# The b projection of a gated convolution as seven-product pairs, in one chain of nine pairs with c and h

## The chip, the cores and the metric

The kernel runs on one core of one Trainium2 chip. The metric is the device time of one execution in microseconds, the median of several runs. One execution was also taken by the hardware profiler; all rows of the profile come from that one.

## The reference, cut to what matters

One decoder layer. 576 tokens (512 new positions of one prompt, and 8 sequences of 8 sample positions) of width 1024 are normalised and go through one wide projection `w_in`, whose 6144 columns are six parts of 1024. The change touches the first three, b, c and h:

```python
xn = rms_norm(h, g_mix[i])
z = xn @ w_in[i]
b, c, hc = z[..., :o1], z[..., o1:o2], z[..., o2:o3]
...
u = c * h
ext = jnp.concatenate([buf, u], axis=1)
y = sum(ext[:, k:k + T] * w_conv[k] for k in range(CONV_W))
return b * y, ext[:, -(CONV_W - 1):]
```

The product b * y is then projected by `w_out_conv`, gated, added to a pooled branch and projected again; an MLP of width 4096, a gated per-layer embedding and a last normalisation follow. Everything is float32.

## The kernel before, in words

**Layout.** Channels lie on the 128 partitions, tokens along the free dimension, in two halves of 288 (256 prompt and 32 sample tokens). There are NJ = 8 tiles of 128 channels, so a projection of 1024 columns is 8 output tiles, each summing over 8 input tiles. `xg` is the input times the gain; the per-token factor of the normalisation, `r1` (and `r1s`, its square, where c and h meet), is multiplied in after the matmuls.

**Precision.** A float32 operand is split into a high part, rounded to the matmul's type, and the remainder (`split`, lines 87 to 99): ScalarE makes `hi` (L93), VectorE `lo` (L94). A product is then three matmuls, hi x hi, hi x lo and lo x hi. Weights are loaded by SP into `raw` buffers (8 of them, `raw_tile`, L126 to L129), split into 7 pairs of weight buffers (`wsp`, NF = 7), and used in the order of one long list, `order`; `Stream` (L190) loads six items ahead of the splits, and splits as far ahead as the seven buffers allow.

**Plain product.** `product` (L118) makes one output tile from two list items (`unit`, each 128x512 of weights): 8 input tiles x 3 matmuls x 2 halves = 48 matmuls of 128x288, into two of six PSUM banks.

**Seven-product pair.** `Pair` (L155) takes two output tiles q and q + 4 with the two halves of the input channels and the two halves of the tokens as a 2 x 2 by 2 x 2 block product, done with seven quarter products in place of eight (the Strassen-Winograd form). The weight side needs seven matrices, the `forms` a, b, d, s0, s1, s2 and s3. Of these s1 and s0 are sums made by a DMA that adds into a loaded buffer: SP loads `c`, and POOL issues a second DMA that accumulates (`summed`, L162 to L165). s2 and s3 are made by VectorE from buffers that are already there (L184, L186), and all seven are split. The token side (`xo`, an `Operand`) is prepared once. `quarter` (L382) is one quarter product, 4 x 3 = 12 matmuls. `pairs_of` (L436 to L499) runs a chain of n pairs: per pair the products t2, t3, t1, then b21 (whose corner result is ready first and goes to `corner`), then the first product of the next pair (`begin`) or a `filler`, then t4 and b22, after which `finish` gets the other three results. VectorE joins the products out of PSUM in five additions (L461, L463, L465, L492, L494), ScalarE makes one copy (L441). With `late` the first pair leaves out the last quarter of its first products until later.

**The order.** The Tile framework plans each engine's order from dependencies and a model of times. With `pinned` set, matmuls keep the program's order; the other engines' instructions may be moved, but at run time each engine works through its own list in that fixed order.

**The convolution.** Tiles 0 and 4 are done by plain products (the loop at L588). Then, for q = 1, 2, 3 (L603): one chain of two pairs makes c and h of the tiles q and q + 4. `corner` and `finish` scale c by `r1s` into `conv.lo` and `conv.hi`, multiply h into `u` (a `Conv` object per tile, whose `u` is cleared and filled at its edges by POOL, L534 and L535), and convolve (`convolve`, L554: two copies by POOL, one multiplication by ScalarE, L560, two on VectorE, L562). The b parts of the two tiles are two plain products: the first is the `filler` of the chain, the second follows the chain. `gate` (L566) scales b by `r1`, multiplies by the convolved `cv` and splits the result into `ya_in`, the operand of a later stage. Then come the gate projections in a chain of four pairs and the products with `w_oc`, which read `ya_in`.

Of the kernel before, what the change touches and what calls it, by code (L numbers as in the profile page):

```python
# [7 lines left out]
F32 = mybir.dt.float32  # L8
F32R = mybir.dt.float32r
AF = mybir.ActivationFunctionType  # L10
ALU = mybir.AluOpType

P = 128
D = 1024
NJ = D // P
# [3 lines left out]
NH = 2  # L19
HP = SEQ // NH  # L20
HB = DB // NH
HT = HP + HB * DS
# [15 lines left out]
NQ = NJ // 2  # L38
# [4 lines left out]
def tile_hybrid_step(ctx: ExitStack, tc: tile.TileContext, x, pt, vecs, rc, ident, sconv, spool, w_first, w_in,  # L43
                     w_pool, w_oc, w_o, w_up, w_down, w_pg, w_pp,
                     y_out, ncp, npp, ncs, nps):
    nc = tc.nc
# [13 lines left out]
    tmp, acts2 = pool("tmpx", 4), pool("acts1", 10)  # L60
# [57 lines left out]
    def product(unit, operands, base=0, m=P, step=P):  # L118

        ps = psum.tile([P, NH, 512], F32, tag="ps", name="ps") if banks is None else [bank() for _ in range(NH)]  # L120
        n = len(operands)
        steps(ps, unit, operands, range(n), base, m, step, 0, n - 1)
        return ps
# [95 lines left out]
    def unit(ap, adding=False):  # L219
        return [Part(ap[:, i:i + KH], adding=adding) for i in range(0, ap.shape[1], KH)]  # L220

    order = []
    order += unit(w_in[NJ + NQ]) + unit(w_in[2 * NJ + NQ]) + unit(w_in[NQ])

    def forms(pairs, between=(), after=()):

        out = [Form(pairs[0], "a")]
        for q, p in enumerate(pairs):
            out += [Form(p, n) for n in ("s2", "s0", "s1", "b")]
            out += [Form(pairs[q + 1], "a")] if q + 1 < len(pairs) else list(between)  # L230
            out += [Form(p, n) for n in ("d", "s3")]
        return out + list(after)

    for q in range(1, NQ):
        order += forms([Pair(w_in[i * NJ + q], w_in[i * NJ + NQ + q]) for i in (1, 2)],
                       unit(w_in[q]), unit(w_in[NQ + q]))
    order += forms([Pair(w_in[4 * NJ + q], w_in[4 * NJ + NQ + q]) for q in range(NQ)])
    for j in range(NJ):
        order += unit(w_oc[j])
# [16 lines left out]
    stream = Stream(order)  # L256
# [32 lines left out]
    xg, first = [], []  # L289
    for j in range(NJ):  # L290
        if j == 0:
            hi, lo = (acts.tile([P, NH, HT], F32R, tag="act", name=n) for n in ("hi", "lo"))
            for h in range(NH):
                nc.scalar.mul(hi[:, h], xs[j][:, h], v(G_MIX, j))
                nc.vector.scalar_tensor_tensor(
                    out=lo[:, h], in0=xs[j][:, h], scalar=v(G_MIX, j), in1=as32(hi[:, h]),
                    op0=ALU.mult, op1=ALU.subtract)
# [138 lines left out]
    def pairs_of(n, op, corner, finish, late=False, between=None, filler=None):  # L436


        def copied(pa):
            g = tmp.tile([P, 4, HT], F32, tag="g", name="g", bufs=2)  # L440
            nc.scalar.copy(g[:, 1], pa)  # L441
            return g

        def begin(w):
            pa = bank()
            quarter(pa, w, op.f["b11"], range(NQ), True, True)
            return pa, copied(pa)

        if late:
            w, pa = stream.take()[0], bank()  # L450
            quarter(pa, w, op.f["b11"], range(NQ - 1), True, True)
        else:
            pa, g = begin(stream.take()[0])
        for i in range(n):
            pb, pd, pc = bank(), bank(), bank()
            u = tmp.tile([P, HT], F32, tag="u", name="u", bufs=1)
            todo = ((pb, "t2"), (pd, "t3"), (pc, "t1"))

            def middle(x):
                if x == 0:  # L460
                    nc.vector.tensor_tensor(out=u, in0=pb, in1=g[:, 1], op=ALU.subtract)  # L461
                elif x == 1:
                    nc.vector.tensor_tensor(out=g[:, 2], in0=pd, in1=u, op=ALU.add)  # L463
                else:
                    nc.vector.tensor_tensor(out=g[:, 2], in0=pc, in1=g[:, 2], op=ALU.add)  # L465

            if late and i == 0:
                ws = []
                for x, (o, name) in enumerate(todo):
                    ws += stream.take(live=x + 1)  # L470
                    quarter(o, ws[x], op.f[name], range(NQ - 1), True, True)
                rest = range(NQ - 1, NQ)
                quarter(pa, w, op.f["b11"], rest, False, True)
                g = copied(pa)
                quarter(pd, ws[1], op.f["t3"], rest, False, True)
                quarter(pc, ws[2], op.f["t1"], rest, False, True)
                quarter(pa, stream.take(live=4)[0], op.f["b21"], range(NQ), False, True)
                quarter(pb, ws[0], op.f["t2"], rest, False, True)
                for x in range(3):
                    middle(x)  # L480
            else:
                for x, (o, name) in enumerate(todo):
                    quarter(o, stream.take()[0], op.f[name], range(NQ), True, True)
                    middle(x)
                quarter(pa, stream.take()[0], op.f["b21"], range(NQ), False, True)
            corner(i, g, pa)
            if i + 1 < n:
                after = begin(stream.take()[0])
            elif filler:
                filler()  # L490
            quarter(pd, stream.take()[0], op.f["t4"], range(NQ), False, True)
            nc.vector.tensor_tensor(out=g[:, 3], in0=pd, in1=u, op=ALU.add)  # L492
            quarter(pc, stream.take()[0], op.f["b22"], range(NQ), False, True)
            nc.vector.tensor_tensor(out=g[:, 0], in0=pc, in1=u, op=ALU.add)  # L494
            finish(i, g)
            if i + 1 < n:
                pa, g = after
            if between:
                between(i)  # L499
# [20 lines left out]
    r1, r1s = stat.copies(r, "r", "rs")  # L520

    ncp_t = tmp.tile([P, NJ, CW - 1], F32, tag="ncp", name="ncp_t", bufs=1)
    xo = Operand(10)
# [4 lines left out]
    class Conv:  # L528
# [35 lines left out]
                    op0=ALU.mult, op1=ALU.add)  # L564

        def gate(self, ps):  # L566
            cv = self.cv
            bt = tmp.tile([P, NH, HT], F32, tag="t", name="bt")
            for h in range(NH):
                nc.vector.tensor_tensor(out=bt[:, h], in0=ps[h], in1=r1[:, h], op=ALU.mult)  # L570
            nc.vector.tensor_tensor(
                out=prompt(bt), in0=prompt(bt), in1=cv[:, :SEQ].rearrange("p (h t) -> p h t", h=NH),
                op=ALU.mult)
            nc.vector.tensor_tensor(
                out=sample(bt), in0=sample(bt),
                in1=cv[:, CE:].rearrange("p (b t) -> p b t", b=DB)[:, :, :DS].rearrange(
                    "p (h b) t -> p h b t", h=NH),
                op=ALU.mult)
            ya_in[self.j] = split_act(bt)
# [8 lines left out]
    for j in (0, NQ):  # L588
        ps_c = ps0[0] if j == 0 else product(stream.take(2), xg)
        c = tmp.tile([P, NH, HT], F32, tag="t", name="c")  # L590
# [3 lines left out]
        conv = Conv(j)  # L594
# [5 lines left out]
        differences(j // 2 + 1)  # L600
        conv.gate(ps_b)
    pinned = True
    for q in range(1, NQ):  # L603

        def corner(i, g, c11):
            if i == 0:
                conv.lo = tmp.tile([P, NH, HT], F32, tag="t", name="c")
                nc.vector.tensor_tensor(out=conv.lo[:, 1], in0=c11, in1=r1s[:, 1], op=ALU.mult)
            else:
                conv.now.half(1, c11, conv.lo[:, 1])  # L610

        def finish(i, g):
            if i == 0:
                nc.vector.tensor_tensor(out=conv.lo[:, 0], in0=g[:, 0], in1=r1s[:, 0], op=ALU.mult)
                conv.hi = tmp.tile([P, NH, HT], F32, tag="t", name="c")
                nc.vector.tensor_tensor(out=conv.hi, in0=g[:, 2:4], in1=r1s, op=ALU.mult)
                conv.now = Conv(q)
            else:
                conv.now.half(0, g[:, 0], conv.lo[:, 0])
                conv.now.convolve()  # L620
                conv.then = Conv(q + NQ)
                conv.then.whole(g[:, 2:4], conv.hi)
                conv.now.gate(conv.ps)
                conv.then.convolve()

        def filler():
            conv.ps = product(stream.take(2), xg)

        pairs_of(2, xo, corner, finish, q == 1, filler=filler)
        conv.then.gate(product(stream.take(2), xg))  # L630


    mix = [None] * NJ
# [14 lines left out]
    gates, where, tag = mix, keep, "keep"  # L648
# [6 lines left out]
    gates, where, tag = [None] * NJ, acts, "act"  # L655
    pairs_of(NQ, xo, corner, finish)
    pinned = False
    xo = conv = None
# [4 lines left out]
    tmp = pool("tmpp", 8)  # L663
# [21 lines left out]
    for g, w in reversed(list(enumerate(WINDOWS))):  # L685
        pooled = []
        for i in range(2):
# [7 lines left out]
                out=e[:, PB:PE_].rearrange("p (h t) -> p h t", h=NH),  # L695
                in0=prompt(ps), in1=prompt(r1), op=ALU.mult)
            nc.vector.tensor_tensor(
                out=es[:, :, PB:].rearrange("p (h b) t -> p h b t", h=NH),
                in0=sample(ps), in1=sample(r1), op=ALU.mult)
# [3 lines left out]
            while d < w:  # L703
                q = tmp.tile([P, PEXT], F32, tag="ext", bufs=4, name="q")
                lo = 2 * d - 1
                nc.vector.tensor_tensor(  # L706
                    out=q[:, lo:], in0=s[:, lo:], in1=s[:, lo - d:PEXT - d], op=ALU.add)
# [3 lines left out]
                out=prompt(pl), in0=s[:, PB:PE_].rearrange("p (h t) -> p h t", h=NH),  # L711
                scalar=1.0 / w, in1=e[:, PB:PE_].rearrange("p (h t) -> p h t", h=NH),
                op0=ALU.mult, op1=ALU.subtract)
            nc.vector.scalar_tensor_tensor(
                out=sample(pl),
                in0=s[:, PE_:].rearrange("p (b t) -> p b t", b=DB)[:, :, PB:].rearrange(
                    "p (h b) t -> p h b t", h=NH),
                scalar=1.0 / w,
# [23 lines left out]
    tmp = pool("tmpm", 3)  # L742
# [220 lines left out]
```

## Time and profile before

| what | value |
|---|---|
| median of 3 runs | 888.28 us (888.14 to 888.34) |
| the profiled execution, whole | 886.94 us |
| its span, first to last instruction | 885.1 us |
| mean granted TensorE clock | 0.994 |
| bytes moved by DMA | 111.25 MB, mean 126 GB/s |
| `raw<-w_in` loads issued by SP, by POOL | 104, 28 (256 KB each) |

The span lies 1.84 us inside the profiled execution's own time. PE and PEld are TensorE's matmuls and weight loads, DVE is VectorE, ACT ScalarE, POOL GpSimd, SP SyncE. A group's row gives the code line, the operation, output and inputs, shape and count, then busy time, mean duration and the idle time just before. Matmul records overlap, since the next begins before the last has drained, so a matmul's duration is longer than the time from one to the next.

### The profile page before, as it was taken

What the parts mean: (1) busy time and instruction counts of PE and PEld (TensorE: products, weight loads), DVE (VectorE), ACT (ScalarE), POOL (GpSimd) and SP (SyncE); (2) the same over time, 40 slices, a digit from 0 to 9 for tenths busy, and PEclk for the clock granted to TensorE, in tenths of its full rate; (3) what the DMA queues carried; (4) which work ended last, traced back from release to release, by engine and by line L of the source; (5) the groups of instructions that cost most, each with busy time, mean ns of one, the idle gap of its engine ahead of it and who ended that gap; (6) DMA issues with size and microseconds to landing.
All of it is one profiled execution on the core that took longest, in us unless ns stands there. A gap on an engine that the chain in (4) does not pass through costs nothing.

```text
span 885.1 us, 16776 instructions
## 1 busy us (share of the span) xinstructions
PE 867.9 (98%) x6506; PEld 863.5 (98%) x6506; DVE 594.1 (67%) x1063; ACT 426.5 (48%) x754; POOL 139.5 (16%) x176
## 2 busy tenths in 40 slices
PE   8999999999999999999899999999999999999995
PEld 8999999999999999899899999999999999999995
DVE  7997797974358599768873248535763377687454
ACT  8653343652135555355674247512762167546332
POOL 4212112100010242032200010011001010021353
PEclk9999999999999999999999999999999999999997
DMA  8636546644454776554444454254544454323012
GB/s 261 155 113 148 132 131 159 154 131 116 103 130 133 194 160 134 179 132 107 121 154 116 104 135 128 96 139 101 144 132 117 107 135 132 96 85 108 1 38 71
DMA packets 62160, 111.25 MB, mean 126 GB/s; under 512 B 7296, under 2 KB 11008, under 8 KB 62080
## 3 DMA queue, kind: packets, MB, share of 16 engines
q1 hardware_dynamic: 50992, 90.21, 32.0%
q0 software_dynamic: 10944, 19.93, 14.4%
q8 instruction: 51, 0.84, 0.4%
q14 instruction: 29, 0.24, 0.1%
q10 hardware_dynamic: 144, 0.03, 0.0%
HBM read 107.16 MB, written 2.99 MB: 124 GB/s over the span
## 4 chain that ended last, share of the span: by engine, by line
PE 84%; DVE 9%; issue 3%; DMA 2%; ACT 1%; SPq 0%; POOL 0%; DVEq 0%; POOLq 0%; ACTq 0%
PE b L67 76%; PE psg L67 6%; DVE lo L94 2%; DVE q L706 2%; DMA raw<-w_up 2%; PE psn L340 1%; DMA xin<-x 1%; PE psn L367 1%; ACT hi L93 1%; DVE pl L710 1%; DVE t L679 1%; DVE e L694 0%; DVE t L681 0%; PE ps L67 0%; DVE xall L755 0%
## 5 line engine op out<-in xcount | busy, mean ns | idle before, releaser
L67 PE MATMUL b<-hi 128*128 128x288 f32 x1832 | 461.9, 296 | 4.3 <-DVE t L679 1.6
L67 PE MATMUL b<-lo,hi 128*128 128x288 f32 x1832 | 460.4, 295 | 1.2 <-DVE lo L94 1.1
L67 PE MATMUL b<-hi,lo 128*128 128x288 f32 x1832 | 460.6, 295 | 0.6 <-DVE lo L94 0.6
L67 PEld LDWEIGHTS b<-hi 128*128 128x128 f32 x1832 | 317.6, 188 | 6.7 <-DVE t L679 1.8
L67 PEld LDWEIGHTS b<-lo,hi 128*128 128x128 f32 x1832 | 317.6, 188 | 1.8 <-DVE lo L94 1.6
L67 PEld LDWEIGHTS b<-hi,lo 128*128 128x128 f32 x1832 | 317.5, 188 | 0.9 <-DVE lo L94 0.8
L93 ACT CAST hi<-raw 128x512 fp32r<-128x512 f32 x288 | 177.0, 621 | 266.3 <-PE b L67 253.8
L94 DVE TENSOR_TENSOR lo<-raw,hi 128x512 fp32r<-128x512 f32 x288 | 202.8, 708 | 102.4 <-ACT hi L93 98.2
L164 POOL DMA_DIRECT2D raw<-w_up x32 | 28.1, 878 | 334.5 <-DMA raw<-w_up 151.7
L329 POOL TENSOR_TENSOR sq<-sq 128x576 f32<-128x576 f32 (+2 forms) x32 | 41.6, 1301 | 112.1 <-ACT sq L323 63.4
L93 ACT CAST hi<-s 128x512 fp32r<-128x512 f32 x60 | 37.0, 618 | 45.9 <-PE b L67 41.3
L94 DVE TENSOR_TENSOR lo<-s,hi 128x512 fp32r<-128x512 f32 x60 | 41.2, 688 | 20.3 <-ACT hi L93 18.9
L164 POOL DMA_DIRECT2D raw<-w_in x28 | 24.4, 870 | 183.7 <-DVE lo L94 71.5
L184 DVE TENSOR_TENSOR s<-raw 128x512 f32<-128x512 f32 x30 | 20.7, 690 | 45.5 <-DMA raw<-w_up 28.9
L67 PE MATMUL psg<-hi 128*128 128x320 f32 (+1 forms) x128 | 38.1, 298 | 0.0
L67 PE MATMUL psg<-lo,hi 128*128 128x320 f32 (+1 forms) x128 | 37.9, 296 | 0.0
L67 PE MATMUL psg<-hi,lo 128*128 128x320 f32 (+1 forms) x128 | 37.9, 296 | 0.0
L67 PE MATMUL ps<-lo,hi 128*128 128x288 f32 x160 | 34.4, 296 | 0.0
L67 PE MATMUL ps<-hi 128*128 128x288 f32 x160 | 34.2, 296 | 0.1
L67 PE MATMUL ps<-hi,lo 128*128 128x288 f32 x160 | 34.2, 296 | 0.0
L94 DVE TENSOR_TENSOR lo<-g,hi 128x576 fp32r<-128x576 f32 x32 | 26.3, 834 | 6.6 <-ACT hi L93 6.6
L811 DVE TENSOR_TENSOR acc<-b,acc 128x288 f32<-128x288 f32 x48 | 19.8, 450 | 15.1 <-PE b L67 15.1
(132 smaller groups left out, 803.4 us busy)
## 6 DMA issues: line engine op xcount, KB each, us to landing
raw<-w_in SPq DMA_DIRECT2D x104, 256.0 KB, 3.0
raw<-w_up SPq DMA_DIRECT2D x80, 256.0 KB, 2.9
raw<-w_down SPq DMA_DIRECT2D x64, 256.0 KB, 2.9
raw<-w_up POOLq DMA_DIRECT2D x32, 256.0 KB, 4.3
raw<-w_in POOLq DMA_DIRECT2D x28, 256.0 KB, 4.6
raw<-w_oc SPq DMA_DIRECT2D x16, 256.0 KB, 2.8
raw<-w_o SPq DMA_DIRECT2D x16, 256.0 KB, 3.5
raw<-w_pg SPq DMA_DIRECT2D x16, 256.0 KB, 2.9
```

Source lines behind the costliest of these rows:

```text
L67: i = nc.tensor.matmul(*args, **kw)
L93: nc.scalar.copy(hi, src)
L94: nc.vector.tensor_tensor(out=lo, in0=src, in1=as32(hi), op=ALU.subtract)
L164: nc.gpsimd.dma_start(raw, y, accum_op=ALU.add)
L184: nc.vector.tensor_tensor(out=p.rs2, in0=p.rs1, in1=p.ra, op=ALU.add)
L329: nc.gpsimd.tensor_tensor(out=self.parts[0], in0=self.parts[0], in1=sq, op=ALU.add)
L340: nc.tensor.matmul(sums[:, i:i + 1], a[:, h, c:c + m], ones32[:, 0:1], start=k == 0, stop=k == len(self.parts) - 1)
L367: nc.tensor.matmul(self.ps[:, h, c:c + m], self.y[:, i:i + 1].broadcast_to([m, P]), idt[:m, :m], start=True, stop=True)
L679: nc.vector.scalar_tensor_tensor(out=t, in0=halves(ps), scalar=v(P_SCALE, j), in1=gates[j], op0=ALU.mult, op1=ALU.mult)
L706: nc.vector.tensor_tensor(out=q[:, lo:], in0=s[:, lo:], in1=s[:, lo - d:PEXT - d], op=ALU.add)
L710: nc.vector.scalar_tensor_tensor(out=prompt(pl), in0=s[:, PB:PE_].rearrange("p (h t) -> p h t", h=NH), scalar=1.0 / w, in1=e[:, PB:PE_].re ...
L811: nc.vector.tensor_tensor(out=accs[j][:, h], in0=ps[h], in1=accs[j][:, h], op=ALU.add)
```

## The change

For q = 1, 2, 3 the b parts of the tiles q and q + 4 are made by a seven-product pair too. The list of weights and the three chains of two pairs with two plain products each become one chain of nine pairs, in the order c, h, b for each q. `corner` and `finish` work out q and the part from the pair's number. The first tile's `Conv` is made in the corner of the h pair instead of at the end of the c pair; the second tile is convolved right after the first; both tiles are gated at the end of the b pair. `gate` is cut in two, the second half being `gated`. In the b pair one quarter comes out with its sign turned, hence the scalar -1. The tiles 0 and 4 stay as they were.

```diff
-    for q in range(1, NQ):
-        order += forms([Pair(w_in[i * NJ + q], w_in[i * NJ + NQ + q]) for i in (1, 2)],
-                       unit(w_in[q]), unit(w_in[NQ + q]))
+    order += forms([Pair(w_in[i * NJ + q], w_in[i * NJ + NQ + q]) for q in range(1, NQ) for i in (1, 2, 0)])
...
         def gate(self, ps):
-            cv = self.cv
             bt = tmp.tile([P, NH, HT], F32, tag="t", name="bt")
             for h in range(NH):
                 nc.vector.tensor_tensor(out=bt[:, h], in0=ps[h], in1=r1[:, h], op=ALU.mult)
+            self.gated(bt)
+
+        def gated(self, bt):
+            cv = self.cv
...
-    for q in range(1, NQ):
-
-        def corner(i, g, c11):
-            if i == 0:
...
-        def finish(i, g):
...
-                conv.now = Conv(q)
-            else:
-                conv.now.half(0, g[:, 0], conv.lo[:, 0])
-                conv.now.convolve()
-                conv.then = Conv(q + NQ)
-                conv.then.whole(g[:, 2:4], conv.hi)
-                conv.now.gate(conv.ps)
-                conv.then.convolve()
-
-        def filler():
-            conv.ps = product(stream.take(2), xg)
-
-        pairs_of(2, xo, corner, finish, q == 1, filler=filler)
-        conv.then.gate(product(stream.take(2), xg))
+
+    def corner(i, g, c11):
+        q, part = i // 3 + 1, i % 3
+        if part == 0:
+            conv.lo = tmp.tile([P, NH, HT], F32, tag="t", name="c")
+            nc.vector.tensor_tensor(out=conv.lo[:, 1], in0=c11, in1=r1s[:, 1], op=ALU.mult)
+        elif part == 1:
+            conv.now = Conv(q)
+            conv.now.half(1, c11, conv.lo[:, 1])
+        else:
+            conv.bt = tmp.tile([P, NH, HT], F32, tag="t", name="bt")
+            nc.vector.tensor_tensor(out=conv.bt[:, 1], in0=c11, in1=r1[:, 1], op=ALU.mult)
+
+    def finish(i, g):
+        q, part = i // 3 + 1, i % 3
+        if part == 0:
...
+        elif part == 1:
+            conv.now.half(0, g[:, 0], conv.lo[:, 0])
+            conv.now.convolve()
+            conv.then = Conv(q + NQ)
+            conv.then.whole(g[:, 2:4], conv.hi)
+            conv.then.convolve()
+        else:
+            nc.vector.scalar_tensor_tensor(
+                out=conv.bt[:, 0], in0=g[:, 0], scalar=-1.0, in1=r1[:, 0], op0=ALU.mult, op1=ALU.mult)
+            conv.now.gated(conv.bt)
+            bt = tmp.tile([P, NH, HT], F32, tag="t", name="bt")
+            nc.vector.tensor_tensor(out=bt, in0=g[:, 2:4], in1=r1, op=ALU.mult)
+            conv.then.gated(bt)
+
+    pairs_of(3 * (NQ - 1), xo, corner, finish, True)
```

More of the change, by code (lines that the diff above doesn't have):

```diff
@@ L602, in tile_hybrid_step @@
     pinned = True
-    for q in range(1, NQ):
-        def corner(i, g, c11):
-            if i == 0:
-                conv.lo = tmp.tile([P, NH, HT], F32, tag="t", name="c")
-                nc.vector.tensor_tensor(out=conv.lo[:, 1], in0=c11, in1=r1s[:, 1], op=ALU.mult)
-            else:
-                conv.now.half(1, c11, conv.lo[:, 1])
-        def finish(i, g):
[L613 to L616, printed above, removed]
-                conv.now = Conv(q)
-            else:
-                conv.now.half(0, g[:, 0], conv.lo[:, 0])
-                conv.now.convolve()
-                conv.then = Conv(q + NQ)
-                conv.then.whole(g[:, 2:4], conv.hi)
-                conv.now.gate(conv.ps)
-                conv.then.convolve()
-        def filler():
-            conv.ps = product(stream.take(2), xg)
-        pairs_of(2, xo, corner, finish, q == 1, filler=filler)
-        conv.then.gate(product(stream.take(2), xg))
+    def corner(i, g, c11):
[9 more added lines that the diff above has]
+            nc.vector.tensor_tensor(out=conv.bt[:, 1], in0=c11, in1=r1[:, 1], op=ALU.mult)
@@ new lines, in finish @@
+    def finish(i, g):
+        q, part = i // 3 + 1, i % 3
+        if part == 0:
+            nc.vector.tensor_tensor(out=conv.lo[:, 0], in0=g[:, 0], in1=r1s[:, 0], op=ALU.mult)
+            conv.hi = tmp.tile([P, NH, HT], F32, tag="t", name="c")
+            nc.vector.tensor_tensor(out=conv.hi, in0=g[:, 2:4], in1=r1s, op=ALU.mult)
+        elif part == 1:
[11 more added lines that the diff above has]
+            conv.then.gated(bt)
```

## The prediction

> **What bounds the kernel now.** I read the page's table of engines first, then the chain that ended last, then the stages one by one.
>
> ```profile
> PE 867.9 (98%) x6506; PEld 863.5 (98%) x6506; DVE 594.1 (67%) x1063; ACT 426.5 (48%) x754; POOL 139.5 (16%) x176
> ...
> PE 84%; DVE 9%; issue 3%; DMA 2%; ACT 1%; SPq 0%; POOL 0%; DVEq 0%; POOLq 0%; ACTq 0%
> ```
>
> TensorE is busy for 98% of the span and makes 84% of the last chain, but these are averages over stages. The change lies in the convolution, so the chain in order of time around it comes next:
>
> ```profile
> 30.66 0.47 DVE c L592
> 31.18 25.05 PE b L67 x186
> 56.24 0.40 ACT g L441
> 56.68 239.73 PE b L67 x1803
> ```
>
> From 31.2 to 296.4 us the chain is matmuls and nothing else but one 0.40 us copy. 239.73 us over 1803 matmuls is 0.133 us each. Then the stages (columns: us, and the busy time and instructions of PE, PEld, DVE, ACT and POOL, the granted clock, the DMA engines' share, GB/s):
>
> ```profile
> core 0: us, PE busy (x) PEld busy (x) DVE busy (x) ACT busy (x) POOL busy (x), PEclk, DMA share, GB/s
> 31.20:50.40 19.20, 19.20 (x144) 19.20 (x145) 18.80 (x39) 11.10 (x19) 4.75 (x10) 1.00 0.44 116
> 50.40:85.60 35.20, 35.12 (x264) 34.73 (x263) 28.60 (x58) 14.43 (x25) 5.09 (x10) 1.00 0.56 143
> 85.60:120.80 35.20, 35.20 (x268) 35.20 (x268) 28.61 (x56) 14.92 (x25) 6.13 (x14) 1.00 0.52 136
> 120.80:156.00 35.20, 35.20 (x268) 35.20 (x268) 28.50 (x56) 14.77 (x26) 7.09 (x12) 1.00 0.54 141
> 156.00:200.80 44.80, 44.80 (x339) 44.80 (x339) 38.06 (x71) 25.12 (x46) 2.60 (x3) 1.00 0.51 144
> 200.80:252.00 51.20, 51.20 (x386) 51.20 (x385) 19.30 (x37) 11.16 (x19) 4.32 (x5) 1.00 0.45 109
> ```
>
> The three rows of 35.20 us are the loop over q = 1, 2, 3 that the change rewrites. By the code one turn has 264 matmuls (two pairs of 84 and two products of 48); the rows show up to four more, those cut by the window's ends. So a turn runs at 35.20 / 264 = 0.133 us a matmul. That PE is "busy" proves little, since its ends are modelled; the pace does. Between 200.8 and 252.0 us VectorE has only 19.30 us of work in 51.20 and the pace is the same (386 in 51.20, again 0.133). It is TensorE's own pace, and in the loop nothing slows it. So **TensorE bounds the loop, by the number of matmuls**, with VectorE at 28.6 of 35.2 us as the next engine.
>
> **The change part by part.**
>
> *Matmuls.* A pair of output tiles by plain products is 2 x 8 x 3 x 2 = 96 matmuls; by seven quarter products of 4 x 3 it is 7 x 12 = 84. Shapes are alike (128x288 moving). Three pairs lose 12 each: 36 x 0.133 = **4.8 us** less, the loop from 105.6 to 100.8 us (33.6 a turn).
>
> *VectorE.* Here lies the price. The rows of one turn, by shape (columns: line, operation, count, busy, mean ns, idle before):
>
> ```profile
> L94 DVE TENSOR_TENSOR lo<-raw,hi 128x512 fp32r<-128x512 f32 x14 | 9.6, 683 | 1.0 <-ACT hi L93 0.7
> ...
> L570 DVE TENSOR_TENSOR bt<-b,r 128x288 f32<-128x288 f32 x4 | 1.6, 448 | 0.0
> ...
> L184 DVE TENSOR_TENSOR s<-raw 128x512 f32<-128x512 f32 x2 | 1.4, 692 | 4.7 <-DMA raw<-w_in 4.7
> L186 DVE SCALAR_TENSOR_TENSOR s<-s,raw 128x512 f32<-128x512 f32 x2 | 1.4, 686 | 0.0
> ...
> L492 DVE TENSOR_TENSOR g<-b,u 128x288 f32<-128x288 f32 x2 | 0.9, 458 | 0.4 <-PE b L67 0.3
> ...
> L465 DVE TENSOR_TENSOR g<-b,g 128x288 f32<-128x288 f32 x2 | 0.9, 447 | 0.0
> L616 DVE TENSOR_TENSOR c<-g,rs 128x576 f32<-128x576 f32 x1 | 0.8, 751 | 0.0
> ```
>
> A b pair needs seven split weights in place of four: three more `lo` at 0.683, one `s2` at 0.692, one `s3` at 0.686, and five sums out of PSUM (lines 461 to 494) at 0.447 to 0.458. That is 2.05 + 0.69 + 0.69 + 2.26 = 5.7 us. The scaling of b by r1 goes from four halves at 0.448 to two halves and one whole at 0.751: 0.14 less. So 5.55 us a turn by durations. Neighbours overlap, though, as the timeline shows (start, duration):
>
> ```profile
> 92.98 0.45 DVE L465 TENSOR_TENSOR g<-b,g 128x288 f32<-128x288 f32 x1
> 93.35 0.68 DVE L94 TENSOR_TENSOR lo<-raw,hi 128x512 fp32r<-128x512 f32 x1
> 93.95 0.68 DVE L186 SCALAR_TENSOR_TENSOR s<-s,raw 128x512 f32<-128x512 f32 x1
> 94.55 0.45 DVE L608 TENSOR_TENSOR c<-b,rs 128x288 f32<-128x288 f32 x1
> ```
>
> From start to start a 512-wide one takes 0.60 and a 288-wide one 0.37, so the five and the five take 3.0 + 1.85 = 4.85, less 0.07 for the scaling: 4.8. The 28.6 of the window is a union of overlapping spans, so 4.8 is the number to add to it: **33.4 us of VectorE in a turn of 33.6 us**; with 5.55 it would be 34.2. VectorE goes from 81% to 99% of the turn. Whether that costs time hangs on the weights split ahead, which the waits of 20 to 200 us show:
>
> ```profile
> ACT hi L93 <- PE b L67: 65.6, 64, 2.6
> ...
> DVE s L184 <- DMA raw<-w_in: 12.9, 5, 4.9
> ```
>
> Sixty-four times ScalarE's split waited for TensorE to give up a weight buffer, so the seven buffers (NF) are mostly full: one in use, six ahead. In the new chain each lasts 12 matmuls, 1.6 us, so the **lead is up to 9.6 us**. The c pair is lighter on VectorE than the h pair, which carries the convolution, and the b pair, which carries the gating: 0.2 us of balance in a turn is lent within it from that lead. After the loop come four pairs with 38.06 of 44.80 us, which pay off what is left. So I take **nothing** for VectorE, with a loss of 3 x (34.2 - 33.6) = 1.8 us as the upper end if the lead is not there, before any wait. The cover is the lead; if it goes, every us of VectorE's idle time is a us of the end.
>
> *ScalarE.* Three more splits and one more copy a turn:
>
> ```profile
> L93 ACT CAST hi<-raw 128x512 fp32r<-128x512 f32 x14 | 8.7, 621 | 12.6 <-PE b L67 12.0 <-ACT g L441 0.7
> ...
> L441 ACT COPY g<-b 128x288 f32<-128x288 f32 x2 | 0.8, 394 | 0.0
> ```
>
> 3 x 0.621 + 0.394 = 2.3 us on 14.9 of 35.2: hidden behind the matmuls.
>
> *DMAs.* A b pair had four loads by SP; now it has five, and two accumulating ones that POOL issues after the SP load below them has landed: in all three SP loads and six POOL ones more, 256 KB each.
>
> ```profile
> raw<-w_in SPq DMA_DIRECT2D x43, 256.0 KB, 3.2
> raw<-w_in POOLq DMA_DIRECT2D x13, 256.0 KB, 5.2
> ```
>
> 3.2 and then 5.2 us are 8.4 us one behind the other, against a pair of 11.2 us and loads that run six forms ahead of the splits. The DMA engines are at 0.52 to 0.56 and would gain 2.36 MB in 100 us, some 23 GB/s on 140. POOL's queue holds the u tiles' clearing and filling and the copies of the states between such issues, so these start later; they are needed by the convolution, not by a matmul. The wait added is `s2` on the accumulated sum: behind it on VectorE stand the splits and the PSUM sums of the running pair, and for those TensorE waits once the lead is used up. It is not taken as free below.
>
> *Moves.* The first tile's Conv goes from the end of the c pair to the corner of the h pair, and both gatings to the end of the b pair; they feed the products from 200.8 us on. PSUM: six banks in turn, four a pair; `pd` reuses the bank that the corner read 48 matmuls (6.4 us) before. No cost taken. The three restarts of a short chain fall away; TensorE lost nothing there (35.20 of 35.20), so no gain either.
>
> *A rule against it.* In the trace a POOL copy next to VectorE's work is sometimes long, and in another stage a VectorE subtraction is:
>
> ```profile
> 82.23 0.19 POOL L535 COPY u<-sc 128x16 f32<-128x16 f32 x1
> ...
> 85.65 0.70 POOL L535 COPY u<-sc 128x16 f32<-128x16 f32 x1
> ...
> 435.41 2.46 DVE L94 TENSOR_TENSOR lo<-g,hi 128x576 fp32r<-128x576 f32 x1
> ...
> 435.47 3.68 POOL L329 TENSOR_TENSOR sq<-sq 128x576 f32<-128x576 f32 x2
> ```
>
> The Trainium skill, "SBUF — State Buffer", section "Who interferes with whom", says that a VectorE instruction with two SBUF inputs and a GpSimd instruction that reads SBUF exclude each other for their whole length. By that rule the five added 512-wide instructions a turn could each be held by a POOL copy, and the loss would be that of the second rival below; the trace agrees at 435.41, beside POOL's additions, but not in this loop, where the 14 subtractions have a mean of 683 ns.
>
> *Sum.* The profiled execution took 886.94 us, 1.84 more than its span: 886.94 - 4.8 = 882.1. The median of the runs is 1.34 above the profiled one, so **883.5** for the median.
>
> **The rivals.**
>
> *First, VectorE ends last.* For it: 33.4 to 34.2 of 33.6 us. If 0.5 us a turn of short waits remain and the lead counts for nothing, the loop takes 3 x 34.7 = 104.1 us, saving 1.5: **886.8**. Against it: the window of 31.2 to 50.4, where VectorE is at 18.80 of 19.20 and TensorE loses nothing.
>
> *Second, slower: the sums arrive late.* `s2` stands in VectorE's fixed order and can wait there for POOL's DMA with all else behind it:
>
> ```profile
> 74.04 0.69 DVE L184 TENSOR_TENSOR s<-raw 128x512 f32<-128x512 f32 x1 [4.85 <-DMA raw<-w_in]
> ...
> 103.21 0.69 DVE L184 TENSOR_TENSOR s<-raw 128x512 f32<-128x512 f32 x1 [2.66 <-DMA raw<-w_in]
> ...
> 108.19 0.69 DVE L184 TENSOR_TENSOR s<-raw 128x512 f32<-128x512 f32 x1 [2.00 <-DMA raw<-w_in]
> ...
> 410.00:433.00 23.00, 21.32 (x153) 20.24 (x152) 19.44 (x36) 15.38 (x28) 2.98 (x4) 1.00 0.48 123
> 433.00:450.00 17.00, 15.89 (x123) 15.49 (x122) 14.90 (x23) 12.00 (x22) 4.16 (x3) 1.00 0.50 150
> ```
>
> Two pairs a turn wait 4.66 us here; three would wait 7.0. Then a turn needs 40.4 us, 6.8 too many; three turns 20.4, less a lead of 9.6: 10.8 late, against 4.8 saved: **894.3**. It turns to slower where the wait passes about 5.6 us a turn (3 x (33.4 + 5.6 - 33.6) - 9.6 = 6.6, which is 4.8 and the 1.8 that a measurement can tell). For it: from 410 to 450 us TensorE loses 2.8 us at the start of such a chain, with VectorE at 85 to 88%. Against it: the four pairs from 156 us run without a loss, and a VectorE that is behind comes to `s2` later, when the sum has landed. The Trainium skill, "TensorE: Matmul & The Clock Gate", section "Part 1: The HAM clock gate", has an idle stretch of about 3.4 us halve TensorE's clock; the 2.8 us lost in pieces left the granted clock at 1.00, which agrees, and a single longer stretch would make this rival dearer.
>
> *Third, the rest of the kernel shifts.* The order on each engine is planned anew, and stages after the loop may gain or lose about what TensorE idles there, 1 to 3 us either way: 882 to 886.
>
> **How the numbers follow.** Forecast 0.64 (TensorE bound, under 1 us lost), first rival 0.17, second 0.09, third 0.10. A measurement of this kernel can tell about 0.2%, 1.8 us, from no change, so faster ends at 886.5. Faster: the forecast, most of the third and a third of the first, 0.74; within: 0.14; slower: the second and strays, 0.12. The range goes from 882.0 (a small gain by the third) to 888.5 (the first rival with waits at a before-like 4.5 us a turn: 3 x 4.3 - 9.6 = 3.3 lost, and a little more); outside remain the second rival and strays, under 2 in 10.
>
> **What would show it.** Right: 6470 matmuls, all in a loop of about 100.8 us with PE at full in every turn; VectorE 1063 + 27 = 1090 instructions and at 98% or more of the loop; `raw<-w_in` 107 by SP and 34 by POOL. First rival: VectorE full, splits no longer waiting for PE, and PE's pace over 0.133. Second: gaps of PE behind `lo` L94, with `s` L184 waiting for a DMA just before. Wrong altogether: a pace other than 0.133 without any idle PE.

## The result, and the profile after

The changed kernel takes **893.16 us** (median of 4 runs, 891.70 to 893.63) against 888.21 before (4 runs, 887.77 to 888.34): 1.0061 times as long, 95% interval 1.0041 to 1.0081. Forecast were 883.5 and a range of 882.0 to 888.5. It is slower, by almost exactly as much as it was to be faster.

The profiled execution took 891.70 us, 4.76 more than the one before. The counts are those of the prediction (first part of the page; then its DMA issues):

```profile
PE 868.0 (98%) x6470; PEld 863.3 (97%) x6470; DVE 606.1 (68%) x1090; ACT 430.1 (48%) x766; POOL 143.6 (16%) x182
...
raw<-w_in SPq DMA_DIRECT2D x107, 256.0 KB, 3.2
...
raw<-w_in POOLq DMA_DIRECT2D x34, 256.0 KB, 4.6
```

So the 36 matmuls are gone, and 4.8 us with them; some 9.5 us have come in. Counted by matmuls, the stretch from the 300th matmul to the one that was the 1500th before (from 42.7 to 202.3 us there) took 159.55 us before and takes 164.93 now, 5.4 more in place of 4.8 less. The loss lies in the loop, and its windows show where (columns as before: us, busy time and instructions of PE, PEld, DVE, ACT, POOL, clock, DMA share, GB/s):

```profile
core 0: us, PE busy (x) PEld busy (x) DVE busy (x) ACT busy (x) POOL busy (x), PEclk, DMA share, GB/s
...
90.00:96.00 6.00, 5.15 (x39) 4.95 (x38) 6.00 (x14) 4.77 (x9) 0.86 (x1) 1.00 0.50 136
...
114.00:120.00 6.00, 4.64 (x36) 4.44 (x35) 5.42 (x10) 2.64 (x5) 2.15 (x6) 1.00 0.28 51
...
130.00:132.00 2.00, 1.15 (x9) 0.94 (x8) 2.00 (x5) 2.00 (x5) 0.49 (x1) 1.00 0.44 73
...
148.00:152.00 4.00, 4.00 (x32) 4.00 (x31) 1.52 (x3) 0.07 (x1) 0.86 (x1) 1.00 0.39 84
152.00:154.00 2.00, 0.30 (x3) 0.07 (x1) 2.00 (x6) 1.30 (x2) 1.28 (x4) 1.00 0.85 138
154.00:156.00 2.00, 0.00 (x0) 0.00 (x0) 2.00 (x5) 0.68 (x1) 1.04 (x2) 1.00 0.42 128
156.00:158.00 2.00, 1.77 (x8) 1.77 (x9) 2.00 (x4) 1.14 (x3) 0.00 (x0) 0.64 0.11 33
158.00:160.00 2.00, 2.00 (x11) 2.00 (x10) 2.00 (x5) 0.62 (x1) 0.00 (x0) 0.50 0.41 131
```

TensorE, full in every such row before, now has holes: 0.85 + 1.36 + 0.85 us at 95, 117 and 131, and 3.93 us from 152 to 156. From 156 to 160 it runs, but the granted clock is 0.64 and 0.50 and only 19 matmuls stand where 30 would. The row to read beside the big hole is 148 to 152: there VectorE works for 1.52 of 4.00 us. An engine that was to fill 99% of the turn stood still just before TensorE did. Its timeline says for what (start, duration, instruction, idle time before it and its releaser):

```profile
78.30 0.69 DVE L184 TENSOR_TENSOR s<-raw 128x512 f32<-128x512 f32 x1 [1.85 <-issue]
...
114.58 0.69 DVE L184 TENSOR_TENSOR s<-raw 128x512 f32<-128x512 f32 x1 [3.21 <-issue]
...
150.48 0.69 DVE L184 TENSOR_TENSOR s<-raw 128x512 f32<-128x512 f32 x1 [4.86 <-DMA raw<-w_in]
151.09 0.45 DVE L492 TENSOR_TENSOR g<-b,u 128x288 f32<-128x288 f32 x1
...
152.50 0.45 DVE L459 TENSOR_TENSOR u<-b,g 128x288 f32<-128x288 f32 x1
...
155.73 0.45 DVE L461 TENSOR_TENSOR g<-b,u 128x288 f32<-128x288 f32 x1
```

Once a turn, 36 us apart, VectorE waits at an `s2`. Where the row says "issue" the releaser is the same: the sums' DMAs landed at 78.22 and 114.50 us, 0.08 us before. It is never the `s2` that is due: counted through the list, those at 78.30, 114.58 and 150.48 belong to the fifth, eighth and eleventh pair (from the tenth on they are those of the gate projections), while VectorE is just finishing the second, fifth and eighth. They are made two pairs early, 22.6 to 25.5 us before VectorE's first sum of their own pair, and block what is due. The chain that ended last goes the same way, from the sum's DMA to TensorE:

```profile
143.99 6.41 DMA raw<-w_in
...
150.48 0.69 DVE s L184
...
155.81 0.38 DVE g L461
...
156.23 3.91 PE b L67 x16
```

After the wait VectorE still has the convolution's work in its fixed order before L461 (L463 in the old numbering), which reads the bank `pd`. The next matmuls, t4, add into that bank and stand still until it has been read:

```profile
152.01 0.29 PE L67 MATMUL b<-hi,lo 128*128 128x288 f32 x1
156.23 0.40 PE L67 MATMUL b<-hi 128*128 128x288 f32 x1 [3.93 <-DVE g L461]
```

The hole of 1.36 us at 117 is a wait for L461 too. Two more profiles of the changed kernel, those of runs 5 and 9 below, have the same list of instructions on every engine and the same big hole: 3.92 and 4.09 us, with waits of 4.84 and 5.02 us at that `s2`.

The small holes at 95 and 131 come by another way, ScalarE:

```profile
84.45 0.62 ACT L93 CAST hi<-raw 128x512 fp32r<-128x512 f32 x1 [0.63 <-PE b L67]
90.93 0.68 ACT L93 CAST hi<-bt 128x576 fp32r<-128x576 f32 x1 [5.86 <-DVE bt L575]
91.72 0.62 ACT L93 CAST hi<-s 128x512 fp32r<-128x512 f32 x1
...
93.34 2.18 ACT L93 CAST hi<-raw 128x512 fp32r<-128x512 f32 x4
```

Its next instruction is the split of a gated tile, which VectorE has not finished; for 5.86 us the splits of the weights stand behind it, and TensorE has used up its lead.

### The profile page after: what moved, and what is told of

The parts are those of the page before. It is cut to its first block, busy times and chain, and to the rows that moved or that the text cites. A ratio compares the mean times of both kernels' runs of the same rounds, so it can differ in the third digit from the quotient of the medians.

```text
span 889.9 us, 16783 instructions
## 1 busy us (share of the span) xinstructions
PE 868.0 (98%) x6470; PEld 863.3 (97%) x6470; DVE 606.1 (68%) x1090; ACT 430.1 (48%) x766; POOL 143.6 (16%) x182
## 4 chain that ended last, share of the span: by engine, by line
PE 71%; DVE 9%; issue 2%; DMA 1%; ACT 1%; POOL 0%; DVEq 0%; ACTq 0%; POOLq 0%
PE b L67 64%; PE psg L67 6%; DVE q L713 2%; DVE lo L94 2%; DMA raw<-w_in 1%; ACT hi L93 1%; DVE pl L717 1%; DMA raw<-w_up 1%; DVE t L686 1%; PE psn L365 1%; DVE e L701 0%; PE psn L338 0%; DVE t L688 0%; PE ps L67 0%; DVE gt L429 0%
## 5 line engine op out<-in xcount | busy, mean ns | idle before, releaser
L67 PE MATMUL b<-hi 128*128 128x288 f32 x1820 | 468.3, 297 | 10.5 <-DVE g L461 5.3
L67 PE MATMUL b<-hi,lo 128*128 128x288 f32 x1820 | 466.2, 296 | 0.5 <-DVE lo L94 0.5
L67 PE MATMUL b<-lo,hi 128*128 128x288 f32 x1820 | 465.5, 296 | 0.6 <-DVE lo L94 0.6
L93 ACT CAST hi<-s 128x512 fp32r<-128x512 f32 x66 | 40.5, 618 | 45.9 <-PE b L67 29.8
L164 POOL DMA_DIRECT2D raw<-w_in x34 | 29.5, 868 | 200.7 <-DVE lo L94 103.3
L94 DVE TENSOR_TENSOR lo<-s,hi 128x512 fp32r<-128x512 f32 x66 | 45.0, 686 | 20.5 <-ACT hi L93 19.0
L184 DVE TENSOR_TENSOR s<-raw 128x512 f32<-128x512 f32 x33 | 22.7, 688 | 45.9 <-DMA raw<-w_up 30.5
```

The lines of the kernel that those rows point to most:

```text
L67: i = nc.tensor.matmul(*args, **kw)
L93: nc.scalar.copy(hi, src)
L94: nc.vector.tensor_tensor(out=lo, in0=src, in1=as32(hi), op=ALU.subtract)
L164: nc.gpsimd.dma_start(raw, y, accum_op=ALU.add)
L184: nc.vector.tensor_tensor(out=p.rs2, in0=p.rs1, in1=p.ra, op=ALU.add)
```

## The experiments

Two theories. **A**: the late sum; `s2`, placed too early in VectorE's fixed order, waits for an accumulating DMA. **B**: VectorE is simply full. The twelve runs were taken in three comparisons of four, each with the kernel before beside them. The median of the kernel before was 887.35, 887.86 and 887.77 us there, and single times lie further apart than in the first comparison (885.0 to 893.0).

**1. One buffer for s2 (changed kernel).** With one, `s2` of a pair cannot be placed before `s3` of the pair ahead is split.

```diff
-                p.rs2 = tmp.tile([P, KH], F32, tag="s", name="s2", bufs=2)
+                p.rs2 = tmp.tile([P, KH], F32, tag="s", name="s2", bufs=1)
```

> The changed kernel with one buffer for the summed weights s2 and s3 in place of two, so that VectorE's s2 of a pair can't be planned before s3 of the pair ahead is split. The work is the same. Theory A (a late sum: s2 stands in VectorE's fixed order up to two pairs before its use and waits there for the accumulating DMA, and TensorE runs dry behind it): the waits of L184 in the loop go, TensorE's gaps of 31 to 300 us go, and the time is 883.5 to 885. Theory B (VectorE is simply full, 33.4 to 34.2 us of work in 33.6 a turn): the time stays at 892 to 894, with the gaps at other places.

Measured: **880.68 us, 0.9924** (0.9899 to 0.9949) of the kernel before. In its timeline none of the twelve `s2` from 50 to 200 us has idle time before it, and the loop is nearly full (its windows):

```profile
50.40:84.00 33.60, 33.52 (x251) 33.06 (x250) 30.62 (x61) 15.78 (x29) 6.95 (x13) 1.00 0.58 142
84.00:117.50 33.50, 33.50 (x255) 33.50 (x254) 32.55 (x65) 15.75 (x28) 7.89 (x14) 1.00 0.69 166
117.50:151.00 33.50, 32.29 (x244) 32.08 (x243) 32.00 (x63) 15.21 (x27) 7.16 (x12) 1.00 0.66 166
```

As A has it, and more: it is below the range that A gave. What the excess is, the third run shows.

**2. The same work without the wait (changed kernel).**

```diff
-                nc.vector.tensor_tensor(out=p.rs2, in0=p.rs1, in1=p.ra, op=ALU.add)
+                nc.vector.tensor_tensor(out=p.rs2, in0=p.ra, in1=p.ra, op=ALU.add)
```

> The changed kernel, two buffers as it was, but s2 is made from the plainly loaded a twice in place of the accumulated s1 and a: the same VectorE instructions and the same DMAs, only s2 no longer has to wait for an accumulating DMA (this leaves out the true s2, and with it the products that use it). Theory A: the waits at L184 go and the time is 883.5 to 885.5. Theory B: 892 to 894, as the work is the same.

Measured: 878.74 us, 0.9902 (0.9879 to 0.9925), also below A's range. Its windows:

```profile
84.00:117.50 33.50, 33.50 (x255) 33.50 (x254) 32.53 (x65) 16.07 (x28) 7.12 (x14) 1.00 0.71 165
117.50:151.00 33.50, 33.50 (x255) 33.50 (x254) 33.13 (x66) 15.84 (x27) 6.61 (x12) 1.00 0.69 169
```

This is the clearest of the runs. All but 7 of VectorE's 1090 instructions stand in the same order as in the changed kernel. VectorE works for 33.13 of 33.50 us, and TensorE does not miss one; counted by matmuls as above, the stretch takes 154.96 us, 4.6 less than before the change. VectorE at 99% costs nothing; the wait does. B, as an account of the change, falls.

**3. One buffer, kernel before**, the control.

> The kernel before with one buffer for s2 and s3. The control: theory A says that its waits at L184 in the convolution loop (9.5 us in sum over the pairs) cost nothing since TensorE never ran dry there, so 887.5 to 888.5; waits at the start of the later chains may move by 1 us. Theory B: no change either, 888.2.

Measured: 883.70 us, 0.9962 (0.9941 to 0.9983): faster by 3.65 us, where both theories had no change. The loop is as full as it was (159.44 us counted by matmuls). The gain lies at the start of the MLP's first chain, where TensorE had lost 2.8 us (windows of the kernel before, then of this one):

```profile
410.00:460.00 50.00, 47.21 (x351) 45.73 (x350) 41.26 (x76) 36.14 (x64) 7.14 (x7) 1.00 0.47 134
```

```profile
410.00:460.00 50.00, 49.94 (x380) 49.39 (x379) 41.46 (x75) 34.28 (x62) 6.69 (x6) 1.00 0.48 134
```

The kernel before waits at two `s2` there or just ahead (its timeline):

```profile
395.88 0.69 DVE L184 TENSOR_TENSOR s<-raw 128x512 f32<-128x512 f32 x1 [5.59 <-DMA raw<-w_up]
...
433.83 0.69 DVE L184 TENSOR_TENSOR s<-raw 128x512 f32<-128x512 f32 x1 [2.54 <-DMA raw<-w_up]
```

With one buffer there is no such wait from 375 to 445 us. The same early `s2` cost time there all along; so part of the first run's gain is not the change's.

**4. One buffer, nine load buffers (changed kernel).**

```diff
-    wraw = ctx.enter_context(tc.tile_pool(name="wraw", bufs=8))
+    wraw = ctx.enter_context(tc.tile_pool(name="wraw", bufs=9))
```

> As the first one, with nine load buffers in place of eight (the room of the freed one). Theory A: as the first one, 883.5 to 885. A third theory, C (it is the loads that are short, the sums landing late because eight load buffers are too few for five loads a pair): the first one keeps half of the loss or more (888 to 891) and this one is faster than it by 1 us or more.

Measured: 881.44 us, 0.9930 (0.9909 to 0.9951), no faster than the first. C falls.

**5. The changed kernel again.**

> The changed kernel itself, beside the others on one chip. It gave 893.2 against 888.2 before; here about 5 us above the kernel before again, and 11 to 12 above the one-buffer version if theory A holds.

Measured: 890.77 us, 1.0034 (1.0014 to 1.0054): 2.9 us above the kernel before, less than the 5 that I expected, and 10.1 above the one-buffer version, whose time is of another comparison.

**6. One buffer for s2, four for u and cv.**

```diff
-            self.u = tmp.tile([P, CEXT], F32, tag="ext", bufs=3, name="u")
+            self.u = tmp.tile([P, CEXT], F32, tag="ext", bufs=4, name="u")
...
-            self.cv = cv = tmp.tile([P, CEXT], F32, tag="ext", bufs=3, name="cv")
+            self.cv = cv = tmp.tile([P, CEXT], F32, tag="ext", bufs=4, name="cv")
```

> The one-buffer version of the changed kernel with four buffers for u and cv in place of three. Theory A: what is left in its loop is one gap of 1.4 us at 149 us, behind POOL's filling of u, which waits for a buffer; it goes, and the time is 1 to 2 us less than with three. Theory B: VectorE's work is the same, so no change.

A miss: 882.54 us, 0.9928 (0.9908 to 0.9948), and the hole is still there, larger. Its chain that ended last runs through VectorE's own convolution work:

```profile
146.04 0.58 POOL u L533
...
146.65 0.80 ACT cv L558
...
147.47 0.84 DVE cv L560
...
148.83 0.83 DVE cv L560
149.66 0.38 DVE g L461
...
150.08 2.05 PE b L67 x7
```

POOL filled `u` at the same time as with three buffers, and with the fourth the planner put L461 behind two more L560: with three buffers it stands ahead of these two, at 146.47. My reading of that hole, a wait of POOL for a buffer, was wrong.

**7. One buffer, every s2 made twice.**

```diff
                 nc.vector.tensor_tensor(out=p.rs2, in0=p.rs1, in1=p.ra, op=ALU.add)
+                nc.vector.tensor_tensor(out=p.rs2, in0=p.rs1, in1=p.ra, op=ALU.add)
```

> The one-buffer version with every s2 made twice over: one more 512-wide VectorE instruction a pair, 3 x 0.60 = 1.8 us a turn, so 33.1 + 1.8 = 34.9 us of VectorE in a turn of 33.5. Theory B in its weak form (work beyond the turn is paid in full): 3 x 1.4 = 4.2 us slower than the one-buffer version. Theory A with the cover of the splits ahead: 0 to 2 us slower.

Measured: 890.87 us, 1.0011 (0.9991 to 1.0031), some 10 us above the one-buffer version, more than either theory gave. No `s2` waits for a DMA; a sum out of PSUM is late at the loop's end, and the clock falls behind it. Its windows, and below them that of the one-buffer version:

```profile
20.00:33.00 13.00, 13.00 (x91) 13.00 (x90) 9.31 (x21) 6.84 (x13) 2.02 (x3) 0.74 0.70 186
...
150.00:180.00 30.00, 26.49 (x181) 26.29 (x180) 28.07 (x53) 14.10 (x24) 5.20 (x10) 0.89 0.59 149
```

```profile
150.00:180.00 30.00, 29.24 (x220) 29.27 (x221) 28.44 (x56) 16.67 (x31) 3.45 (x4) 1.00 0.64 160
```

From 150 to 180 us 39 matmuls fewer are done, 5.2 us; 3.51 of them are one wait for L462 (L461, its number here one higher), the rest mostly the clock. From 60 to 150 us 13 fewer are done (1.7 us), and a clock of 0.74 at the start of the span, where the one-buffer version's profile has 1.00 and 110 matmuls, is 19 more (2.5 us). So B is wrong of the change and right of the limit: some 33 us of work in a turn of 33.5 are free, with 3 x 0.69 us more VectorE falls behind and is paid for. The drop at the start is not this edit's: the second profile of the one-buffer version (run 10) has 0.74 and 91 matmuls there too. Counted by matmuls, the loop's stretch takes 163.90 us here, against 156.53 and 156.69 in the two profiles of the one-buffer version: some 7.3 of the 10 us lie in the loop, the clock that falls behind the wait included.

**8. The gated tile's high part by POOL (changed kernel, two buffers).**

```diff
-            ya_in[self.j] = split_act(bt)
+            hi, lo = (acts.tile([P, NH, HT], F32R, tag="act", name=n) for n in ("hi", "lo"))
+            nc.gpsimd.tensor_copy(hi, bt)
+            nc.vector.tensor_tensor(out=lo, in0=bt, in1=as32(hi), op=ALU.subtract)
+            ya_in[self.j] = hi, lo
```

> The changed kernel with two buffers for s2, where the high part of the gated tiles is made by POOL in place of ScalarE. Theory A in full: the late s2 has two ways to TensorE, by ScalarE, whose queue stands at the gated tile's split (5.9 us at 85 to 91 us) with the weights' splits behind it, and by the sums out of PSUM. Then the gaps at 94 and 130 us (1.1 us each) go and those at 117 and 152 us stay: 889 to 892, 2 to 3 us under the changed kernel. If the weights' splits are held up by VectorE itself, 893.

A miss that tells nothing of ScalarE's part: 901.55 us, 1.0146 (1.0108 to 1.0183). It moved the instruction into a queue that is worse, POOL's, whose accumulating DMAs wait for loads, and VectorE then waited for POOL (waits from 50 to 200 us):

```profile
PE b L67 <- DVE g L461: 11.8, 3, 4.2
POOL hi L581 <- DVE bt L575: 10.5, 2, 6.1
...
DVE lo L582 <- POOL hi L581: 6.9, 3, 3.4
```

**9 to 12. All in one comparison**, on one chip.

> The changed kernel once more, for one comparison of all on one chip: 890 to 893, 2 to 5 us above the kernel before.

> The changed kernel with one s buffer once more: 880 to 882.5. What tells the theories apart is its distance from the kernel before with one s buffer in this same call: theory A, 36 matmuls fewer (4.8 us) less the 1.3 us more that its loop loses: 3 to 4 us faster than it. Theory B: no faster than it.

> The kernel before with one s buffer once more: 883 to 885, from the start of the MLP's first chain, not from the convolution, whose loop lost nothing before.

> The kernel before with s2 made from a twice (this leaves out the true s2), so that no s2 waits for an accumulating DMA. Theory A: nothing changes from 31 to 297 us, where TensorE never ran dry; what is gained lies at the start of the MLP's chain (up to 4 us): 883 to 886. A theory D (s2's waits cost TensorE something before the change too): more than 1 us less between 31 and 297 us.

The last one is the edit of the second run in the kernel before. Its time ended 0.5 us under its range, the others inside theirs.

| kernel | median us | of the kernel before, 95% interval |
|---|---|---|
| before | 887.77 | 1 |
| changed | 892.35 | 1.0036 (1.0016 to 1.0056) |
| before, one s buffer | 883.19 | 0.9956 (0.9939 to 0.9973) |
| changed, one s buffer | 880.11 | 0.9915 (0.9892 to 0.9939) |
| before, s2 from a twice | 882.48 | 0.9944 (0.9924 to 0.9964) |

With two buffers the change costs 4.6 us; with one it gains 883.19 - 880.11 = 3.1 us. The two versions of the change have the same matmuls and the same work; what differs is VectorE's order, in which some 60 of 1090 instructions stand elsewhere. That it is the place of `s2` that decides rests on the second run, where the wait alone goes. The last row has 100.52 busy us of TensorE from 50.4 to 151 us, as has the kernel before: before the change `s2` cost the loop nothing, and D falls. **The version with the change and one buffer beats both kernels by a clear margin.**

## Why the prediction was wrong, point by point

*TensorE bounds the loop, 36 matmuls are worth 4.8 us*: right. Where nothing waits (second run) the loop runs at TensorE's pace, and its stretch of 1200 matmuls is 4.6 us shorter for the 36 that are gone; the one-buffer pair of kernels shows 3.1 us.

*VectorE goes to 33.4 us of 33.6*: right in size (32.53 and 33.13 of 33.50 in the second run's last two turns), and right that this alone costs nothing.

*"So I take nothing for VectorE ... The cover is the lead"*: this step failed. The term put at nothing cost some 10 us: the loop's stretch came out 5.4 us longer instead of 4.8 shorter, and the second run, without the wait, has 4.6 of these 4.8. The lead of 9.6 us is that of split weights. But TensorE asks VectorE for a second thing, the sums out of PSUM, and there the cover is less: between t3, whose result L461 reads, and t4, which adds to the same bank, stand three products (t1, b21, the next pair's first), 36 x 0.133 = 4.8 us. The biggest hole, 3.93 us, is a wait for L461, not for weights. "No cost taken" for PSUM looked at banks in turn and overlooked the one used twice.

*That waits of such length had been harmless before* misled me. The wait of 4.85 us at 74.04 in the kernel before fell behind the sums that t4 and b22 need (L463 and L465, which are L461 and L463 after the change):

```profile
67.32 0.45 DVE L463 TENSOR_TENSOR g<-b,u 128x288 f32<-128x288 f32 x1
...
68.73 0.46 DVE L465 TENSOR_TENSOR g<-b,g 128x288 f32<-128x288 f32 x1 [0.34 <-PE b L67]
74.04 0.69 DVE L184 TENSOR_TENSOR s<-raw 128x512 f32<-128x512 f32 x1 [4.85 <-DMA raw<-w_in]
...
78.94 0.45 DVE L492 TENSOR_TENSOR g<-b,u 128x288 f32<-128x288 f32 x1
```

For 10 us after them no PSUM sum was due, since the filler, a plain b product of 48 matmuls (6.4 us), stood between b21 and t4. In the changed kernel the wait of 4.86 us stands ahead of the running pair's sums (L459 at 152.50, L461 at 155.73), and the filler is gone. It was computing and perhaps cushion at once, and I counted only the first. No run put a filler back, so that this is what made the old waits harmless is a reading of the two traces; two shorter waits that stood ahead of such sums before, 2.66 us at 103.21 and 1.60 at 137.10, cost TensorE nothing either.

*The second rival* named the mechanism (the sums arrive late, in VectorE's fixed order, slower) and came within 1.1 us of the time, 894.3 against 893.16, with a chance of 0.09. That it came so near is luck. It took 7.0 us of waiting a turn, 21 in all, and paid 9.6 of them from the lead; the trace has 9.9 us of waits in all, which the lead did not pay for, and the holes stand behind L461 and ScalarE's `hi`, not behind `lo`. Its point of decision, 5.6 us of waiting a turn, was wrong with the lead in it: 1.85, 3.21 and 4.86 us were enough. *"A VectorE that is behind comes to s2 later, when the sum has landed"* failed too, since a VectorE that had more to do than before still waited 4.86 us. A likely reason, which no run tests: load buffers are given back by VectorE's and ScalarE's splits, so a late VectorE makes the sums late as well (waits of the changed kernel from 50 to 200 us; the first row was 5.8 us in two waits before the change):

```profile
POOL raw L164 <- DVE lo L94: 31.0, 6, 6.6
...
POOL raw L164 <- DMA raw<-w_in: 29.6, 7, 6.4
```

*The rule on the clock*, weighed there: the Trainium skill, "TensorE: Matmul & The Clock Gate", section "Part 1: The HAM clock gate", has TensorE's clock fall to half after an idle window of about 3.4 us, and come back after a busy one of that length. Here the trace agrees: after the hole of 3.93 us some 15 matmuls come 0.24 us apart, 1.6 us lost on top. But less than an idle window was enough elsewhere, as the last section shows. *The rule on the shared port* (the Trainium skill, "SBUF — State Buffer", section "Who interferes with whom") had no part: the holes have waits behind them, not long instructions, and VectorE's 128x512 subtractions of loaded weights took 679 ns in the mean from 60 to 160 us, against 683 in a turn before.

What stays open: whether ScalarE's standing at the gated tile alone would hold TensorE up once `s2` is in place, since the run meant for it did not test it.

## What to carry to other kernels

Before an engine is filled to 99%, list every hand-off by which the bounding engine waits for it, and take the shortest cover, not the one that is easiest to see. An instruction placed early in a fixed order is harmless only as long as its input is there in time, or nothing behind it is due; one buffer fewer can be the way to keep a planner from hoisting it. Work that looks replaceable, like a plain product between two dependent steps, may be what hides the other engines' waits.

## What the runs showed of the hardware that I had not expected

The clock drops after much less idle time than in the hole of 3.93 us, and not each time. Before the last pooled stage ends TensorE is idle for 1.5 us or so in both kernels (windows of the kernel before, then of the changed one):

```profile
354.00:363.00 9.00, 7.32 (x50) 6.40 (x49) 8.95 (x18) 3.86 (x8) 0.00 (x0) 1.00 0.39 125
363.00:367.00 4.00, 4.00 (x30) 4.00 (x31) 3.99 (x6) 1.22 (x2) 0.00 (x0) 1.00 0.14 54
```

```profile
360.00:368.00 8.00, 6.53 (x44) 5.61 (x42) 7.96 (x16) 3.49 (x7) 0.00 (x0) 1.00 0.39 135
368.00:372.00 4.00, 3.62 (x16) 3.62 (x17) 3.99 (x7) 0.81 (x2) 0.00 (x0) 0.57 0.20 63
```

The clock stayed at 1.00 in the one and fell to 0.57 over four microseconds in the other. The clock records of the fourteen profiles tell the two apart. Drops to half last 3.41 or 6.83 us, but for the one at the span's end, and within one profile they begin whole multiples of 3.41 us apart (in the changed kernel at 156.57, 368.20 and 880.20 us, 62 and 150 such steps). With time cut into these steps, 26 matmuls start in a full one. From 30 us on, a step at full clock in which 10 or fewer started was followed by half clock each time, 28 times; with 11 this happened four times in five; with 12 to 15 never, in 17 steps. So what counts is how much of the idle time falls into one step: in the changed kernel 9 matmuls started in the step before 368.20 us, while in the kernel before the same stage has no step with fewer than 12. That is a rule read off these profiles, not a test of it.

A second kind of drop has no idle time just before it. At the very start of the span, from 20 to 33 us, the seventh run's profile has 0.74 and 91 matmuls, the kernel before 1.00 and 110; TensorE is busy without a break there. Five of the fourteen profiles have such a drop, whatever the edit, and no run shows its cause.

A drop costs about half of its length, 1.7 or 3.4 us. Single times of one kernel go with the clock: of the 29 runs of the kernel before in the last comparison the fastest, 885.18 us, has a mean granted clock of 0.995 and the slowest, 893.03, one of 0.984. A profile should be searched for such drops before two executions are compared.
